# Gate factors over all vg steps, normalisation between the Strassen pairs, spatial weights early, output products fed block by block

## The chip, the cores and the metric

The kernel runs on one core of a Trainium2 chip. The metric is the device time of one execution in microseconds; the time given for a kernel is the median of its runs. The engines are named as the profile names them: PE is TensorE, DVE is VectorE, ACT is ScalarE, POOL is GpSimd, SP is SyncE. Each works through its own instructions in the order in which they stand in its stream.

## The reference

One layer of a hybrid trunk, with S = 512 tokens, D = 2048 channels, all in fp32:

```python
h = rms_norm(x, g_mix)
q, k, v_sb, u, v_sg, gate_a, gate_b = split(h @ w_in)      # 3 x 1024, 2 x 1024, 2 x 2048 columns
y_a = stick_breaking_attention(rms_norm(q), rms_norm(k), v_sb) @ w_oa     # 8 heads of 128
u = gelu(u); v_sg = gelu(v_sg)
v = layer_norm(v_sg, ln_g, ln_b)
mixed = einsum('gij,bcjgd->bcigd', masked(w_s), v) + b_s    # 8 groups, 4 chunks of 128 tokens
y_b = (u * mixed) @ w_ob
x = x + (sigmoid(gate_a) * y_a + sigmoid(gate_b) * y_b) @ w_out
x = x + square(relu(rms_norm(x, g_ff) @ w_ff1)) @ w_ff2
```

## The kernel before

**Products.** Every fp32 operand is split into a high and a low part (`split`, `split_to`, `weight`: ACT casts the high part, DVE subtracts to get the low part), and a product is three matmuls (`mm3`, L72 to L74). Weights come in pieces of 512 KB on SP's queue; their parts go into six buffers `w_piece`. Tiles of 128 x 512 come from one pool of slots, `slots`, and a smaller one, `long`; a new tile waits until the last user of an old one is done.

**Stages in order.** `by_token` makes q, k, v, then the vg columns (the gating unit's v), each in two halves of 512 columns; attention of a half runs beside the products that follow it. Then come `plain_pair` (two blocks of u as a plain product) and 19 `strassen_pair` (the rest of u, then both gates), which compute two column blocks by a Strassen scheme with sums of halves of h as moving operands; `factor` makes those sums, the "gate factors". Then `by_column` makes ya (from w_oa) and yb (from w_ob), then the output product and the feed-forward part, which the change leaves alone.

**Order of the work around a product.** A queue `behind` holds functions. After each weight piece `step()` runs the next one; `flush()` runs all that are left. What the functions emit goes to the engines through a scheduler, which sets the final order on each engine; `tc.issue_after(x)` keeps a transfer behind instruction x.

**Names.** `attention(half, ...)` gives 12 steps of `weights(h)` (scores and the weights `beta`), `turn(h)` (transposes `aT` on PE, split into `aT_hi`, `aT_lo`) and `product(h)` (the product `o`, split into `oT_hi`, `oT_lo`, stored to `held_o`). `save` has put h whole into `held_h`. `gate_factors(k)` fetches two tiles `whole` on POOL's queue and makes four sums, each a DVE operation (L241), an ACT one (L107 or L110) and a DVE one (L108 or L111). The evacuation of vg is a Gelu on ACT (L608). `normed(tb)` is the layer norm of 128 tokens: statistics on DVE, multiply and add on POOL (L637, L638), split on ACT and DVE into `vn`, two stores to `held_v` per half. `gated` multiplies a result by the row factor (L647, tile `act`), applies the activation (L648) and stores it to `held_g`. `spatial(half)` transposes four groups of w_s (`wsT`, L685) and splits them. `fetch_mix` fetches vn and u back, `mixed(g)` mixes one group (`mix`, `smix`) and splits it (`sT`). `evac_a` multiplies ya by a gate into `merged_a` (L737), for each of four column blocks; `gates` fetches the four gate tiles of a block.

In vg's 16 steps before, attention of the second half takes 12 and the eight gate factors the last four, two in each:

Of the kernel before, what the change touches and what calls it, by code (L numbers as in the profile page):

```python
# [16 lines left out]
P = 128  # L17
D = 2048
# [17 lines left out]
def tile_hybrid_layer(ctx: ExitStack, tc: tile.TileContext, x, g_mix, w_in, g_q, g_k, ln_g, ln_b,  # L36
# [29 lines left out]
    def f32(ap):  # L66
        return ap.bitcast(F32)
# [19 lines left out]
    def weight(wap, kt, c0, w=W):  # L87

        ck = CK * W // w
        raw = state["raw"].tile([P, ck, w], F32, name="w_raw", tag="w_raw")  # L90
        state["load"] = nc.sync.dma_start(
            out=raw, in_=wap[kt * P:(kt + ck) * P, c0:c0 + w].rearrange("(k p) c -> p k c", p=P))
        hi = wpool.tile([P, ck, w], F32R, name="w_hi", tag="w_piece", bufs=6)
        nc.scalar.copy(out=hi, in_=raw)  # L94
        lo = wpool.tile([P, ck, w], F32R, name="w_lo", tag="w_piece", bufs=6)
        nc.vector.tensor_tensor(out=lo, in0=raw, in1=f32(hi), op=ALU.subtract)  # L96
# [65 lines left out]
    class Sums:  # L162
# [15 lines left out]
        def parts(self, name):  # L178
            if name == "m7":
                nc.vector.tensor_tensor(out=self.a, in0=self.w11, in1=self.w21, op=ALU.add)  # L180
                if self.loaded:
                    nc.gpsimd.dma_start(out=self.w21, in_=self.blocks[1, 1], accum_op=ALU.add)  # L182
# [285 lines left out]

    held_h = dram.tile([KT, P, W], F32, name="held_h")
    held_o = dram.tile([HEADS, 2, P, W], F32, name="held_o")  # L470
    held_v = dram.tile([2, NTB, 2, P, W], F32, name="held_v")
    held_g = dram.tile([(SGW + 2 * D) // P, P, W], F32, name="held_g")
    scale = float(P) ** -0.5

# [110 lines left out]

# [9 lines left out]
    def gate_factors(k):  # L595
        whole = [fetched(held_h[2 * k + i], "whole") for i in range(2)]
        for name in ("m7", "m6", "m4", "m5"):
            factor(hy, whole, k, name, -1.0 if name in ("m7", "m4") else None)

    behind.extend([lambda k=k: (moved(2 * k), moved(2 * k + 1), moved(2 * k + 2), moved(2 * k + 3),  # L600
                                gate_factors(k), gate_factors(k + 1)) for k in range(0, KT // 2, 2)])

    vg = {}
    VS = 3 * SBW + SGW
# [15 lines left out]
                dst.append(t)  # L620
    vn = {}

    def normed(tb):
        st = tiny(12, "st")
        for half in range(2):
            nc.vector.bn_stats(out=st[:, half * 6:half * 6 + 6], in_=vg[tb, half])
# [4 lines left out]
        r = rsqrt(ve, 1, "r")  # L631
        for half in range(2):
            t = vg[tb, half]
            y = slot("y")
            nc.vector.tensor_scalar(out=y, in0=t, scalar1=mv[:, 0:1], scalar2=r, op0=ALU.subtract,
                                    op1=ALU.mult)
            nc.gpsimd.tensor_tensor(out=y, in0=y, in1=lng[half], op=ALU.mult)  # L637
            nc.gpsimd.tensor_tensor(out=y, in0=y, in1=lnb[half], op=ALU.add)  # L638
# [5 lines left out]
    def gated(n, act, func, signs, inside):  # L644
        for c, (t, sign) in enumerate(zip(act, signs)):
            a = t if inside else slot("act")
            nc.vector.tensor_tensor(out=a, in0=t, in1=rstd_b, op=ALU.mult)  # L647
            nc.scalar.activation(out=a, in_=a, func=func, scale=sign)  # L648
            nc.sync.dma_start(out=held_g[n + c], in_=a)

    US, GA = 3 * SBW, 3 * SBW + 2 * SGW
    order = [(US + n * P, n, AF.Gelu) for n in range(0, SGW // P, 2)]
    order += [(GA + n * P, SGW // P + n, AF.Sigmoid) for n in range(0, 2 * D // P, 2)]
    forks = None
    for c0, n, func in order:
        if forks is None:
            gated(n, plain_pair(win, c0, hy, "u"), func, (1.0, 1.0), False)
            flush()
            forks = new_forks(hy["y11", 0])
        else:  # L660
            gated(n, strassen_pair(win, c0, hy, forks), func, SIGNS, True)

    oT = [[fetched(held_o[h, i], "oT", F32R, long if h < LONG // 2 else slots) for i in range(2)]
          for h in range(HEADS)]

    def gates(which, j):
        n = SGW // P + which * (D // P) + j * 4
        return [fetched(held_g[n + c], "gate") for c in range(4)]
# [13 lines left out]
    def spatial(half):  # L682
# [11 lines left out]
        for i in range(2):  # L694
# [36 lines left out]
    ahead = gates(0, 0)  # L731
    for j in range(D // W):
        g, ahead = ahead, gates(0, j + 1) if j + 1 < D // W else gates(1, 0)

        def evac_a(c, o):
            m = slot("merged_a")
            nc.vector.tensor_tensor(out=m, in0=o, in1=g[c], op=ALU.mult)  # L737
# [4 lines left out]
    flush()
    mT = []
    for j in range(D // W):
        g, ahead = ahead, gates(1, j + 1) if j + 1 < D // W else None

        def evac_b(c, o):
            m = slot("merged")
            nc.vector.tensor_tensor(out=m, in0=o, in1=g[c], op=ALU.mult)
# [262 lines left out]
```

## Time and profile before

| | us |
|---|---|
| median of 3 runs | 2493.61 (2493.16 to 2493.72) |
| profiled execution | 2494.17 |
| its span | 2492.4 |
| PE busy in the span | 2428.3 |
| DVE, ACT, POOL busy | 1848.0, 1196.2, 467.9 |
| PE waits of over 1 us in the stages of the change | 18.6, 15.6, 2.6, 2.5, 2.5, 2.2, 2.1, 1.6, 1.1 |

A row of the timeline gives start, duration, engine, line, operation, output and input tiles, and in brackets how long the engine sat idle before it and what ended that. A row of the waits gives the total, how often, and the longest. A row of stretches gives the length, the busy time of PE, PE's weight loads, DVE, ACT and POOL with counts, then the clock granted to PE (1 is full), the busy share of the DMA engines and GB/s. A row of a group gives after the bar the busy time, the mean duration in ns and the idle time before. Stages in the profile of before: vg's second half with attention up to 415 us, u from 415 us, the first Strassen pair from 460 us, ya from 850 us.

### The profile page before, as it was taken

What the parts mean: (1) busy time and instruction counts of PE and PEld (TensorE: products, weight loads), DVE (VectorE), ACT (ScalarE), POOL (GpSimd) and SP (SyncE); (2) the same over time, 40 slices, a digit from 0 to 9 for tenths busy, and PEclk for the clock granted to TensorE, in tenths of its full rate; (3) what the DMA queues carried; (4) which work ended last, traced back from release to release, by engine and by line L of the source; (5) the groups of instructions that cost most, each with busy time, mean ns of one, the idle gap of its engine ahead of it and who ended that gap; (6) DMA issues with size and microseconds to landing.
All of it is one profiled execution on the core that took longest, in us unless ns stands there. A gap on an engine that the chain in (4) does not pass through costs nothing.

```text
span 2492.4 us, 34437 instructions
## 1 busy us (share of the span) xinstructions
PE 2428.3 (97%) x12696; PEld 2087.2 (84%) x12696; DVE 1848.0 (74%) x2416; ACT 1196.2 (48%) x1759; POOL 467.9 (19%) x590
## 2 busy tenths in 40 slices
PE   9999998699999989999999999999999999999999
PEld 7888887589888868888889888889888888888887
DVE  4566465777778644544679888888888899989887
ACT  5333343355555412322457777777765443333333
POOL 0223121610000331300000000000014435312210
PEclk9999999899999989999999999999999999999999
DMA  5243225666666853444459888898895999877763
GB/s 178 93 153 110 87 91 179 171 154 163 157 166 156 263 197 127 144 135 144 122 129 251 222 229 228 223 238 226 228 273 203 329 332 288 248 225 214 247 181 96
DMA packets 446122, 473.64 MB, mean 190 GB/s; under 512 B 20177, under 2 KB 328449, under 8 KB 445953
## 3 DMA queue, kind: packets, MB, share of 16 engines
q1 hardware_dynamic: 355984, 331.95, 41.7%
q0 software_dynamic: 89680, 138.97, 23.5%
q8 instruction: 100, 1.64, 0.3%
q10 hardware_dynamic: 288, 0.52, 0.1%
q14 instruction: 70, 0.57, 0.1%
HBM read 380.13 MB, written 90.18 MB: 189 GB/s over the span
## 4 chain that ended last, share of the span: by engine, by line
PE 61%; DVE 1%; DMA 0%; issue 0%; ACT 0%; POOL 0%; DVEq 0%
PE q L72 9%; PE q L73 9%; PE q L74 9%; PE q L214 7%; PE fork L214 7%; PE fork L217 4%; PE q L217 4%; PE xo L72 2%; PE xo L74 2%; PE xo L73 2%; PE yb L74 1%; PE yb L73 1%; PE yb L72 1%; PE ya L72 1%; PE ya L73 1%; PE ya L74 1%
## 5 line engine op out<-in xcount | busy, mean ns | idle before, releaser
L107 ACT CAST w_hi<-w_raw 128x1024 fp32r<-128x1024 f32 (+1 forms) x576 | 604.8, 1050 | 661.1 <-PE q L73 339.7
L108 DVE TENSOR_TENSOR w_lo<-w_raw,w_hi 128x1024 fp32r<-128x1024 f32 (+1 forms) x576 | 704.9, 1227 | 169.9 <-ACT w_hi L107 160.2
L73 PE MATMUL q<-w_lo,ys 128*128 128x512 f32 x896 | 348.8, 389 | 0.5 <-DVE w_lo L108 0.5
L96 DVE TENSOR_TENSOR w_lo<-w_raw,w_hi 128x1024 fp32r<-128x1024 f32 x135 | 168.9, 1251 | 243.1 <-ACT w_hi L94 239.1
L74 PE MATMUL q<-w_hi,ys 128*128 128x512 f32 x896 | 348.6, 389 | 0.0
L94 ACT CAST w_hi<-w_raw 128x1024 fp32r<-128x1024 f32 x135 | 141.8, 1050 | 373.0 <-issue 78.3
L72 PE MATMUL q<-w_hi,ys 128*128 128x512 f32 x896 | 312.0, 389 | 0.9 <-ACT w_hi L107 0.9
L214 PE MATMUL q<-ys,w_hi 128*128 128x512 f32 x1048 | 268.4, 393 | 2.5 <-ACT fork L221 2.5
L182 POOL DMA_DIRECT2D w_raw<-in_w_ff_dram x58 | 80.9, 1394 | 906.8 <-DVE m L844 343.4
L214 PE MATMUL fork<-ys,w_hi 128*128 128x512 f32 x896 | 224.9, 393 | 0.0
L214 PEld LDWEIGHTS q<-ys,w_hi 128*128 128x128 f32 x1048 | 186.9, 189 | 34.1 <-ACT fork L221 2.7
L73 PEld LDWEIGHTS q<-w_lo,ys 128*128 128x128 f32 x896 | 168.2, 188 | 36.4 <-DVE w_lo L108 1.5
L72 PEld LDWEIGHTS q<-w_hi,ys 128*128 128x128 f32 x896 | 168.1, 188 | 36.2 <-ACT w_hi L107 1.3
L74 PEld LDWEIGHTS q<-w_hi,ys 128*128 128x128 f32 x896 | 168.2, 188 | 34.9
L214 PEld LDWEIGHTS fork<-ys,w_hi 128*128 128x128 f32 x896 | 164.3, 190 | 31.1
L912 POOL DMA_DIRECT2D ys<-store x224 | 128.1, 609 | 175.6 <-PE q L74 117.9
L217 PEld LDWEIGHTS q<-ys,w_lo 128*128 128x128 f32 x1048 | 142.5, 190 | 10.4
L217 PE MATMUL q<-ys,w_lo 128*128 128x256 f32 x1048 | 145.7, 282 | 0.0
L72 PE MATMUL q<-ys,w_hi 128*128 128x256 f32 x400 | 114.4, 286 | 18.6 <-DVE act L647 18.6
L954 DVE SCALAR_TENSOR_TENSOR total<-q,plus,total 128x512 f32<-128x512 f32 x180 | 131.0, 744 | 0.4 <-PE q L74 0.4
L217 PEld LDWEIGHTS fork<-ys,w_lo 128*128 128x128 f32 x896 | 122.3, 190 | 8.6
L217 PE MATMUL fork<-ys,w_lo 128*128 128x256 f32 x896 | 125.3, 282 | 0.0
(293 smaller groups left out, 4732.5 us busy)
## 6 DMA issues: line engine op xcount, KB each, us to landing
w_raw<-in_w_ff_dram SPq DMA_DIRECT2D x256, 512.0 KB, 5.6
w_raw<-in_w_in_dram SPq DMA_DIRECT2D x143, 512.0 KB, 3.9
ys<-store POOLq DMA_DIRECT2D x224, 256.0 KB, 6.8
w_raw<-in_w_ff_dram POOLq DMA_DIRECT2D x58, 512.0 KB, 7.0
store<-ys_hi SPq DMA_DIRECT2D x90, 256.0 KB, 4.5
store<-ys_lo SPq DMA_DIRECT2D x90, 256.0 KB, 5.5
w_raw<-in_w_out_dram SPq DMA_DIRECT2D x32, 512.0 KB, 3.6
store<-ys SPq DMA_DIRECT2D x44, 256.0 KB, 6.3
```

The lines of the kernel that those rows point to most:

```text
L72: nc.tensor.matmul(o, lhsT=lh[0], rhs=rh[0], start=start, stop=False, **kw)
L73: nc.tensor.matmul(o, lhsT=lh[0], rhs=rh[1], start=False, stop=False, **kw)
L74: nc.tensor.matmul(o, lhsT=lh[1], rhs=rh[0], start=False, stop=stop, **kw)
L94: nc.scalar.copy(out=hi, in_=raw)
L96: nc.vector.tensor_tensor(out=lo, in0=raw, in1=f32(hi), op=ALU.subtract)
L107: nc.scalar.copy(out=hi, in_=src)
L108: state["lo"] = nc.vector.tensor_tensor(out=lo, in0=src, in1=f32(hi), op=ALU.subtract)
L182: nc.gpsimd.dma_start(out=self.w21, in_=self.blocks[1, 1], accum_op=ALU.add)
L214: nc.tensor.matmul(o, lhsT=hi[:, k, :], rhs=rhs[name][k], start=name == "y11" and k == 0, stop=False, skip_group_check=True)
L217: nc.tensor.matmul(o[:, :HS], lhsT=lo[:, k, :], rhs=rhs[name][k][:, :HS], start=False, stop=k == KH - 1, skip_group_check=True)
L912: nc.gpsimd.dma_start(out=f32(t), in_=store[f][HELD.index(name), p])
L954: nc.vector.scalar_tensor_tensor(out=a, in0=o, scalar=part, in1=a, op0=ALU.mult, op1=ALU.add)
```

## The change

- The eight gate factors stand at vg's steps 6, 8, 10, 11, 12, 13, 14 and 15, beside attention, which keeps steps 0 to 11; `moved` goes to steps 2 to 5.
- The layer norm is cut in two. `centred` (statistics and scaling, in place in the vg tile) runs for all tokens at u's first step. `normed(tb, half)` is POOL's multiply and add and one store, in every third step of the Strassen pairs. The split into vn parts is done after the fetch (`split_mix`), in ya. `held_v` holds one tile where it held two.
- `spatial` runs at u's third and fourth steps, where it ran at ya's start.
- The oT tiles of two heads are fetched ahead of the last pair, the others behind it into `long`.
- In ya and yb the fetches of vn, u and gates each stand behind a small POOL operation on the low part of the newest weight piece (`let`); `mixed(g)` stands at steps 5 to 8 and 10 to 13, and the flush between ya and yb is gone.

The diff's core (lines of after are one higher from L97 on):

```diff
     def weight(...):
         nc.vector.tensor_tensor(out=lo, in0=raw, in1=f32(hi), op=ALU.subtract)
+        state["piece"] = lo
...
-    held_v = dram.tile([2, NTB, 2, P, W], F32, name="held_v")
+    held_v = dram.tile([2, NTB, P, W], F32, name="held_v")
...
-        behind.extend(attention(half, qT, kT, v))
+        if half == 0:
+            behind.extend(attention(half, qT, kT, v))
...
-    behind.extend([lambda k=k: (moved(2 * k), moved(2 * k + 1), moved(2 * k + 2), moved(2 * k + 3),
-                                gate_factors(k), gate_factors(k + 1)) for k in range(0, KT // 2, 2)])
+    def at_steps(steps):
+        behind.extend([lambda fs=steps.get(i, []): [f() for f in fs] for i in range(max(steps) + 1)])
+
+    steps = collections.defaultdict(list)
+    for i, f in enumerate(attention(half, qT, kT, v)):
+        steps[i].append(f)
+    for k in range(KT):
+        steps[2 + k // 4].append(lambda k=k: moved(k))
+    for k, i in enumerate((6, 8, 10, 11, 12, 13, 14, 15)):
+        steps[i].append(lambda k=k: gate_factors(k))
+    at_steps(steps)
...
-    def normed(tb):
+    def centred(tb):
...
-            y = slot("y")
-            nc.vector.tensor_scalar(out=y, in0=t, scalar1=mv[:, 0:1], scalar2=r, op0=ALU.subtract,
+            nc.vector.tensor_scalar(out=t, in0=t, scalar1=mv[:, 0:1], scalar2=r, op0=ALU.subtract,
                                     op1=ALU.mult)
-            nc.gpsimd.tensor_tensor(out=y, in0=y, in1=lng[half], op=ALU.mult)
-            nc.gpsimd.tensor_tensor(out=y, in0=y, in1=lnb[half], op=ALU.add)
-            for i, part in enumerate(split(y, "vn")):
-                nc.gpsimd.dma_start(out=held_v[half, tb, i], in_=f32(part))
-
-    behind.extend([lambda tb=tb: normed(tb) for tb in range(NTB)])
+    def normed(tb, half):
+        t = vg[tb, half]
+        nc.gpsimd.tensor_tensor(out=t, in0=t, in1=lng[half], op=ALU.mult)
+        nc.gpsimd.tensor_tensor(out=t, in0=t, in1=lnb[half], op=ALU.add)
+        nc.gpsimd.dma_start(out=held_v[half, tb], in_=t)
...
+    behind.extend([lambda: [centred(tb) for tb in range(NTB)], lambda: None, lambda: spatial(0), lambda: spatial(1)])
...
             forks = new_forks(hy["y11", 0])
+            for tb in range(NTB):
+                for half in range(2):
+                    behind.extend([lambda tb=tb, half=half: normed(tb, half), lambda: None, lambda: None])
         else:
+            if (c0, n, func) == order[-1]:
+                with tc.issue_after(state["sum"].ins):
+                    for h in range(2):
+                        fetch_o(h, slots)
             gated(n, strassen_pair(win, c0, hy, forks), func, SIGNS, True)
+    with tc.issue_after(state["sum"].ins):
+        for h in range(2, HEADS):
+            fetch_o(h, long)
...
-            vn[tb, half] = [fetched(held_v[half, tb, i], "vn", F32R) for i in range(2)]
+            vn[tb, half] = fetched(held_v[half, tb], "vn")
...
+    def split_mix(half):
+        for tb in range(NTB):
+            vn[tb, half] = split(vn[tb, half], "vn")
...
-    behind.extend([lambda: (spatial(0), fetch_mix(0)), lambda: spatial(1)])
-    behind.extend([lambda g=g: (mixed(g), fetch_mix(1) if g == 1 else None) for g in range(GROUPS)])
+    def let(f):
+        gate = nc.gpsimd.tensor_tensor(out=tiny(4, "gate"), in0=f32(state["piece"])[:, 0, :4], in1=mhalf,
+                                       op=ALU.mult)
+        with tc.issue_after(gate.ins):
+            f()
+
+    with tc.issue_after(state["sum"].ins):
+        ahead = collections.deque([gates(0, 0)])
+    steps = collections.defaultdict(list)
+    steps[2].append(lambda: let(lambda: fetch_mix(0)))
+    steps[4].append(lambda: split_mix(0))
+    steps[6].append(lambda: let(lambda: fetch_mix(1)))
+    steps[9].append(lambda: split_mix(1))
+    for g in range(GROUPS):
+        steps[5 + g + g // 4].append(lambda g=g: mixed(g))
+    for i, wj in enumerate([(0, 1), (0, 2), (0, 3), (1, 0), (1, 1), (1, 2), (1, 3)]):
+        steps[4 * i].append(lambda wj=wj: let(lambda: ahead.append(gates(*wj))))
+    at_steps(steps)
...
-    flush()
+        ahead.popleft()
```

How the change moves instructions is shown at three places. The first is vg's first half with attention of the second. DVE before, from the last `beta` of `weights(3)` on:

```order
L540 SCALAR_TENSOR_TENSOR rest<-keep 128x128
L544 TENSOR_TENSOR beta<-beta,rest 128x127
L108 TENSOR_TENSOR oT_lo<-o,oT_hi 128x512
L108 TENSOR_TENSOR aT_lo<-aT,aT_hi 128x512
L108 TENSOR_TENSOR aT_lo<-aT,aT_hi 128x384
L108 TENSOR_TENSOR aT_lo<-aT,aT_hi 128x256
L108 TENSOR_TENSOR aT_lo<-aT,aT_hi 128x128
```

DVE now, from the same `beta` on (`whole` and `ys` are the operations of gate factor 0):

```order
L545 TENSOR_TENSOR beta<-beta,rest 128x127
L242 TENSOR_TENSOR whole<-whole 128x256 x2
L112 SCALAR_TENSOR_TENSOR ys<-whole,ys 128x256
L242 TENSOR_TENSOR whole<-whole 128x256
L109 TENSOR_TENSOR ys<-whole,ys 128x256
L242 TENSOR_TENSOR whole<-whole 128x256
L112 SCALAR_TENSOR_TENSOR ys<-whole,ys 128x256
L109 TENSOR_TENSOR ys<-whole,ys 128x256
L109 TENSOR_TENSOR oT_lo<-o,oT_hi 128x512
L109 TENSOR_TENSOR aT_lo<-aT,aT_hi 128x512
L109 TENSOR_TENSOR aT_lo<-aT,aT_hi 128x384
```

The eight DVE operations of factor 0 stand ahead of the `oT_lo` of `product(1)` and the `aT_lo` of `turn(2)`. POOL before, from the last `beta` multiplies of attention (the `whole` fetches are those of factor 0):

```order
L543 TENSOR_TENSOR beta<-beta,past 128x128 x4
L568 DMA held_o<-oT_hi 128x512
L568 DMA held_o<-oT_lo 128x512
L568 DMA held_o<-oT_hi 128x512
L568 DMA held_o<-oT_lo 128x512
L568 DMA held_o<-oT_hi 128x512
L477 DMA whole<-held_h 128x512 x2
```

POOL now, from the same multiplies:

```order
L544 TENSOR_TENSOR beta<-beta,past 128x128 x4
L478 DMA whole<-held_h 128x512 x2
L569 DMA held_o<-oT_hi 128x512
L569 DMA held_o<-oT_lo 128x512
L478 DMA whole<-held_h 128x512 x2
L569 DMA held_o<-oT_hi 128x512
```

The two fetches of factor 0 stand directly behind the last `beta` multiply, where they stood behind five stores of attention. The second place is ACT from u's third weight piece to the first Strassen pair. Before, the cast of that piece (the `w_hi` here) with the factor operations around it:

```order
L110 ACTIVATE ys<-whole 128x256
L107 CAST ys<-whole 128x256
L94 CAST w_hi<-w_raw 128x1024
L110 ACTIVATE ys<-whole 128x256
L107 CAST ys<-whole 128x256
L110 ACTIVATE ys<-whole 128x256
L107 CAST ys<-whole 128x256
```

Now, the casts of u's second and third pieces:

```order
L94 CAST w_hi<-w_raw 128x1024
L111 ACTIVATE ys<-whole 128x256
L94 CAST w_hi<-w_raw 128x1024
L108 CAST ys<-whole 128x256
L111 ACTIVATE ys<-whole 128x256
L108 CAST ys<-whole 128x256
```

The third cast stands inside factor 4, where it stood ahead of the third factor: 24 factor operations on ACT stood behind it before, 15 stand behind it now. Behind them, before, the evacuation of vg's second half and the first part of the pair:

```order
L107 CAST ys<-whole 128x256
L608 ACTIVATE vg<-vg,rstd 128x512 x4
L94 CAST w_hi<-w_raw 128x1024
L107 CAST w_hi<-w_raw 128x1024
L107 CAST vn_hi<-y 128x512
L107 CAST w_hi<-w_raw 128x1024 x2
L107 CAST vn_hi<-y 128x512
L107 CAST w_hi<-w_raw 128x1024
L221 COPY fork<-q 128x512
```

And now:

```order
L108 CAST ys<-whole 128x256
L618 ACTIVATE vg<-vg,rstd 128x512 x4
L94 CAST w_hi<-w_raw 128x1024
L108 CAST w_hi<-w_raw 128x1024 x2
L108 CAST wsp<-wsm 128x2x128
L108 CAST w_hi<-w_raw 128x1024
L108 CAST wsp<-wsm 128x2x128
L108 CAST w_hi<-w_raw 128x1024
L222 COPY fork<-q 128x512
L108 CAST wsp<-wsm 128x2x128 x2
L687 ACTIVATE act<-act 128x512
```

The casts of vn are gone, those of the spatial weights (`wsp`) and the first activation (`act`) stand there. The third place is DVE in ya. Before, at the end of the first column block (`merged_a`):

```order
L108 TENSOR_TENSOR sT_lo<-smix,sT_hi 128x512
L721 TENSOR_TENSOR smix<-mix,bs 128x256 x2
L723 TENSOR_TENSOR smix<-mix,smix 128x256 x2
L108 TENSOR_TENSOR sT_lo<-smix,sT_hi 128x512
L737 TENSOR_TENSOR merged_a<-ya,gate 128x512 x4
L721 TENSOR_TENSOR smix<-mix,bs 128x256 x2
```

And now, at the end of the second:

```order
L109 TENSOR_TENSOR sT_lo<-smix,sT_hi 128x512
L748 TENSOR_TENSOR smix<-mix,bs 128x256 x2
L750 TENSOR_TENSOR smix<-mix,smix 128x256 x2
L109 TENSOR_TENSOR sT_lo<-smix,sT_hi 128x512
L777 TENSOR_TENSOR merged_a<-ya,gate 128x512 x4
L748 TENSOR_TENSOR smix<-mix,bs 128x256 x2
L750 TENSOR_TENSOR smix<-mix,smix 128x256 x2
L109 TENSOR_TENSOR sT_lo<-smix,sT_hi 128x512
```

An `sT_lo` still stands directly ahead of `merged_a` there; at the end of the first block none does.

More of the change, by code (lines that the diff above doesn't have):

```diff
@@ L181, in parts @@
                 if self.loaded:
-                    nc.gpsimd.dma_start(out=self.w21, in_=self.blocks[1, 1], accum_op=ALU.add)
+                    state["sum"] = nc.gpsimd.dma_start(out=self.w21, in_=self.blocks[1, 1], accum_op=ALU.add)
             if name == "m6":
@@ L633, in normed @@
             t = vg[tb, half]
-            y = slot("y")
-            nc.vector.tensor_scalar(out=y, in0=t, scalar1=mv[:, 0:1], scalar2=r, op0=ALU.subtract,
+            nc.vector.tensor_scalar(out=t, in0=t, scalar1=mv[:, 0:1], scalar2=r, op0=ALU.subtract,
                                     op1=ALU.mult)
-            nc.gpsimd.tensor_tensor(out=y, in0=y, in1=lng[half], op=ALU.mult)
-            nc.gpsimd.tensor_tensor(out=y, in0=y, in1=lnb[half], op=ALU.add)
-            for i, part in enumerate(split(y, "vn")):
-                nc.gpsimd.dma_start(out=held_v[half, tb, i], in_=f32(part))
-    behind.extend([lambda tb=tb: normed(tb) for tb in range(NTB)])
[L644 to L657, printed above, removed]
-            flush()
[L659 to L668, printed above, removed]
+    def normed(tb, half):
[3 more added lines that the diff above has]
+        nc.gpsimd.dma_start(out=held_v[half, tb], in_=t)
     wsT = []
@@ L698, in spatial, with gated, fetch_o, gates @@
             wsT.append(pair)
+    def gated(n, act, func, signs, inside):
+        for c, (t, sign) in enumerate(zip(act, signs)):
+            a = t if inside else slot("act")
+            nc.vector.tensor_tensor(out=a, in0=t, in1=rstd_b, op=ALU.mult)
+            nc.scalar.activation(out=a, in_=a, func=func, scale=sign)
+            nc.sync.dma_start(out=held_g[n + c], in_=a)
+    US, GA = 3 * SBW, 3 * SBW + 2 * SGW
+    order = [(US + n * P, n, AF.Gelu) for n in range(0, SGW // P, 2)]
+    order += [(GA + n * P, SGW // P + n, AF.Sigmoid) for n in range(0, 2 * D // P, 2)]
+    behind.extend([lambda: [centred(tb) for tb in range(NTB)], lambda: None, lambda: spatial(0), lambda: spatial(1)])
+    forks = None
+    oT = []
+    def fetch_o(h, pool):
+        oT.append([fetched(held_o[h, i], "oT", F32R, pool) for i in range(2)])
+    for c0, n, func in order:
+        if forks is None:
+            gated(n, plain_pair(win, c0, hy, "u"), func, (1.0, 1.0), False)
+            flush()
+            forks = new_forks(hy["y11", 0])
+            for tb in range(NTB):
+                for half in range(2):
+                    behind.extend([lambda tb=tb, half=half: normed(tb, half), lambda: None, lambda: None])
+        else:
+            if (c0, n, func) == order[-1]:
+                with tc.issue_after(state["sum"].ins):
+                    for h in range(2):
+                        fetch_o(h, slots)
+            gated(n, strassen_pair(win, c0, hy, forks), func, SIGNS, True)
+    with tc.issue_after(state["sum"].ins):
+        for h in range(2, HEADS):
+            fetch_o(h, long)
+    def gates(which, j):
+        n = SGW // P + which * (D // P) + j * 4
+        return [fetched(held_g[n + c], "gate") for c in range(4)]
     sT = []
@@ L725, in mixed @@
         sT.append(split(t, "sT"))
[L727 to L728 removed]
+    def let(f):
[15 more added lines that the diff above has]
+    at_steps(steps)
     merged_a = []
[L731 removed]
     for j in range(D // W):
[L733 removed]
         def evac_a(c, o):
             m = slot("merged_a")
[L737 removed]
+            nc.vector.tensor_tensor(out=m, in0=o, in1=ahead[0][c], op=ALU.mult)
             merged_a.append(m)
         by_column(w_oa[0], j * W, lambda k: oT[k], SBW // P, evac_a, "ya")
[L742 removed]
+        ahead.popleft()
     mT = []
     for j in range(D // W):
[L745 removed]
         def evac_b(c, o):
             m = slot("merged")
[L749 removed]
+            nc.vector.tensor_tensor(out=m, in0=o, in1=ahead[0][c], op=ALU.mult)
             nc.gpsimd.tensor_tensor(out=m, in0=m, in1=merged_a[j * 4 + c], op=ALU.add)
@@ L753, in tile_hybrid_layer @@
         by_column(w_ob[0], j * W, lambda k: sT[k], SGW // P, evac_b, "yb")
+        ahead.popleft()
     EARLY = 6
```

## The prediction

> **What bounds the kernel now.** I read the engine table first, then the list of what TensorE waited for, then the table of stretches with the granted clock, and last the timeline around each long wait. First the span, and the one engine that fills it:
>
> ```profile
> span 2492.4 us, 34437 instructions
> PE 2428.3 (97%) x12696; PEld 2087.2 (84%) x12696; DVE 1848.0 (74%) x2416; ACT 1196.2 (48%) x1759; POOL 467.9 (19%) x590
> ```
>
> TensorE works 97% of the span; 64.1 us of it are idle. The edits take away no large product, so what they can bring is idle time, and matmuls that run at a low clock after it. Who it waits for (total, times, longest):
>
> ```profile
> PE q L72 <- DVE act L647: 18.6, 1, 18.6
> PE u L72 <- ACT vg L608: 15.6, 1, 15.6
> PE ya L72 <- DVE merged_a L737: 5.0, 2, 2.5
> PE mix L717 <- DVE smix L723: 3.9, 2, 2.2
> PE wsT L685 <- DMA ws<-in_w_spatial_dram: 2.6, 1, 2.6
> PE u L72 <- DMA hT<-hT_both: 2.1, 1, 2.1
> PE ya L74 <- DVE w_lo L96: 1.1, 1, 1.1
> ```
>
> These seven, 48.9 us, lie in the code that the change touches. The rest (the first load and single waits elsewhere) is left. After each such wait the same matmuls take longer:
>
> ```profile
> 443.73 0.58 PE L72 MATMUL u<-hT,w_hi 128*128 128x256 f32 x1 [15.60 <-ACT vg L608]
> 449.02 0.30 PE L72 MATMUL u<-hT,w_hi 128*128 128x256 f32 x1
> 449.51 0.28 PE L73 MATMUL u<-hT,w_hi 128*128 128x256 f32 x1
> 449.63 0.28 PE L74 MATMUL u<-hT,w_lo 128*128 128x256 f32 x1
> 927.74 0.80 PE L72 MATMUL ya<-oT,w_hi 128*128 128x512 f32 x1 [2.51 <-DVE merged_a L737]
> 933.45 0.53 PE L73 MATMUL ya<-oT,w_hi 128*128 128x512 f32 x1
> 933.82 0.39 PE L74 MATMUL ya<-oT,w_lo 128*128 128x512 f32 x1
> 430.00:460.00 30.00, 16.27 (x116) 16.27 (x117) 21.66 (x46) 10.58 (x20) 10.70 (x13) 0.72 0.43 107
> 920.00:940.00 20.00, 15.25 (x63) 12.50 (x62) 9.34 (x19) 2.91 (x4) 5.93 (x7) 0.83 0.21 69
> ```
>
> From 443.73 to 449.02 there are 24 matmuls, 0.220 us apart, and then 0.120: 24 x 0.10 = 2.4 us lost after one gap. From 927.74 to 933.82 there are 14 matmuls, 0.43 us apart; with the same near doubling about 0.2 of each is lost, 2.9 in all, though that gap was only 2.51 us. The stretches show it as granted clocks of 0.72 and 0.83. So I price a restart at 2.4. [...]
>
> **Part 1: gate factors over the vg steps.** Before, the eight factors stand after attention, and the evacuation of vg's second half stands on ACT behind the last of them; the second bank of u needs that bank:
>
> ```profile
> 415.08 1.05 ACT L94 CAST w_hi<-w_raw 128x1024 fp32r<-128x1024 f32 x1 [2.72 <-issue]
> 417.31 0.88 DVE L241 TENSOR_TENSOR whole<-whole 128x256 f32<-128x256 f32 x2
> 421.62 0.88 DVE L241 TENSOR_TENSOR whole<-whole 128x256 f32<-128x256 f32 x2
> 443.00 2.41 ACT L608 ACTIVATE vg<-vg,rstd 128x512 f32<-128x512 f32 x4
> ```
>
> One factor is a chain between DVE and ACT of 4.3 us (417.31 to 421.62). Vg's last matmul ends at 415.07 (call it T). In the new order k1 to k3 lie on an idle DVE before T (half busy: 20.3 of 40 us between 360 and 400), but on ACT the w_hi cast of u's third weight, which waits for vg's last matmul, stands in the middle of k4, with the rest of k4 and k5 to k7 behind it. So the evacuation is done at T + 1.05 (that cast) + 2.45 (rest of k4) + 3 x 4.35 + 0.6 (one evacuation) + about 0.5 = T + 17.7, where it was T + 28.7. TensorE now has u's whole first bank ahead of it: 72 matmuls x 0.120 = 8.6. A wait of 9.1 replaces 15.6 + 2.1.
>
> Factor k0 is put earlier than its data allows. On DVE its eight instructions stand behind the last `beta` of `weights(3)` and ahead of the `oT_lo` of `product(1)` and the `aT_lo` of `turn(2)`; its fetch is issued on POOL only behind the last `beta` multiply of `weights(3)`:
>
> ```profile
> 366.11 0.61 POOL L543 TENSOR_TENSOR beta<-beta,past 128x128 f32<-128x128 f32 x1 [1.47 <-ACT beta L536]
> 394.91 1.08 POOL L477 DMA_DIRECT2D whole<-held_h  x2
> 401.37 0.89 DVE L241 TENSOR_TENSOR whole<-whole 128x256 f32<-128x256 f32 x2 [6.56 <-DMA whole<-held_h]
> DMA to landing us min/median/max: 2.7/5.2/6.9
> 368.77 0.68 DVE L108 TENSOR_TENSOR oT_lo<-o,oT_hi 128x512 fp32r<-128x512 f32 x1
> 369.72 0.71 PE L554 MATMUL aT<-ident,beta 128*128 128x128 f32 x3
> 360.00:400.00 40.00, 39.86 (x200) 33.55 (x199) 20.29 (x32) 17.45 (x30) 9.51 (x16) 1.00 0.39 123
> ```
>
> The fourth row is of the `whole` fetches. The second fetch is issued at about 366.72 + 0.54 = 367.3; at 4.5 us (between minimum and median, since only two are sent and DMA is at 0.39) it lands at 371.8, k0 ends at 376.1 and `oT_lo` at 376.8. TensorE wanted to go on with `aT` at 369.72, and the next vg matmuls stand behind `aT` and `o`. That is a new wait of 7.1 us (5.3 with the minimum, 9.5 with the maximum) plus a restart of 2.4: 9.5. This stretch is all busy at full clock before. Together: 17.7 + 9.5 = 27.2 against 28.7, so u's second bank starts 1.5 us earlier. Costs at restart stay: 2.4 before and after.
>
> **Part 2: normalisation, spatial weights, first gating.** Before, q's first product waits 18.6 us, because the `act` multiply stands on DVE behind all eight vn splits, which follow POOL's multiply and add one by one:
>
> ```profile
> 501.76 0.55 PE L72 MATMUL q<-ys,w_hi 128*128 128x256 f32 x1 [18.64 <-DVE act L647]
> L638 POOL TENSOR_TENSOR y<-y,lnb 128x512 f32<-128x512 f32 x8 | 14.1, 1764 | 0.6
> L637 POOL TENSOR_TENSOR y<-y,lng 128x512 f32<-128x512 f32 x8 | 13.2, 1650 | 0.1
> held_v<-vn_hi POOLq DMA_DIRECT2D x8, 256.0 KB, 3.6
> 448.34 1.27 POOL L637 TENSOR_TENSOR y<-y,lng 128x512 f32<-128x512 f32 x1
> 473.26 2.16 POOL L638 TENSOR_TENSOR y<-y,lnb 128x512 f32<-128x512 f32 x1
> ```
>
> The splits go out of this chain, but `act` takes its slot from a vg tile whose store is the second on POOL. Counted from u's second bank (R): first multiply at R + 4.6 (448.34 - 443.73), ten multiplies and adds of 1.79 (mean of the groups with a gap of 0.08), small `r` operations, a weight accumulate and the issues, store at about R + 25, landed 3.6 to 4.2 later at R + 29. Behind it on ACT stand both gating activations and two weight casts; the fork copy that TensorE needs comes at R + 34.5. TensorE gets there at R + 29.8. So a wait of 4.8 (0 to 9), and 1.3 for a shorter restart, in place of 18.6 + 2.4. The eight wsT transposes and the fork work inside u add 1.9. Gain 21.0 - 4.8 - 1.3 - 1.9 = 13.0. The fetch of ws decides a side wait:
>
> ```profile
> ws<-in_w_spatial_dram SPq DMA_DIRECT2D x2, 256.0 KB, 16.8
> xk<-in_x_dram SPq DMA_DIRECT2D x4, 256.0 KB, 5.1
> 850.00:880.00 30.00, 26.32 (x121) 21.37 (x120) 12.85 (x23) 8.37 (x13) 11.82 (x22) 0.94 1.04 383
> ```
>
> The 16.8 us were taken at a DMA share of 1.04; with 0.4 to 0.7 in the new place I take the 5.1 of the other row of 256 KB, which is hidden. The shorter and longer POOL operations (1.27 and 2.16) are the bounds of the chain: ten times 0.4 either way. [...]
>
> **Part 3: the ya products.** Waits before: 2.6 (ws), 1.1 (w_lo), 1.6 and 2.2 (smix), 2.5 and 2.5 (merged_a), 12.5 in sum, and 6.4 at a low clock (2.9 and 2.4 after the `merged_a` gaps, 1.1 after the ws gap, each from the spacing of the matmuls behind it). The ws wait and the smix waits go: the transposes have moved (1.1 of matmul time with them), and `mixed` is spread with empty steps between. The `merged_a` wait stays at two boundaries of column blocks, since `sT_lo`, which waits for ACT, still stands ahead of it on DVE:
>
> ```profile
> 893.29 0.69 DVE L108 TENSOR_TENSOR sT_lo<-smix,sT_hi 128x512 fp32r<-128x512 f32 x1 [2.03 <-ACT sT_hi L107]
> 900.00:920.00 20.00, 20.00 (x97) 16.73 (x96) 8.61 (x14) 5.24 (x6) 4.56 (x6) 1.00 0.56 203
> ```
>
> I leave 2.7 and 1.5 there and 2.1 for the clock. Gain 12.5 + 6.4 + 1.1 - 6.3 = 13.7. The vn splits (8 x 0.7 on DVE, 8 x 0.6 on ACT) fall into the ya stage, where DVE is busy 8.6 of 20 us (last row). Half the vn transfers go, and the oT fetches come earlier; DMA bounds nothing here. The POOL operation that holds back a fetch until a weight's low part is there reads a piece whose buffer is needed three weights later, some 16 us; POOL's work between is under 6 us. Nothing for these.
>
> **Sum.** 1.5 + 13.0 + 13.7 = 28.2. The profiled execution took 2494.17, so 2466.0; it lies 0.56 over the median of 2493.61, so the median becomes 2465.4.
>
> **Rivals.**
> - All waits go: k0's fetch comes in time, the slot is free, the boundaries pass. Then 48.9 of idle and 2.4 + 2.4 + 6.4 of clock, less 1.9 for work moved into u: 2494 - 58 = 2435. Against it stands the order on DVE and ACT.
> - One more wait in u: ws lands after 16.8 as before (about 5.6 more, since the act wait covers a part) or POOL's ten operations take 2.16 each (3.7 more): 2469 to 2475.
> - The early factors cost more: k1's eight instructions stand ahead of a w_lo and of the next `oT_lo`, its fetch behind a store that waits for k0's end. If TensorE runs out of weights there too, another 7.1 + 2.4: 2475, and for k2 as well 2484. The half-busy DVE speaks against it.
> - The factors gain nothing because k0's wait grows to the maximum, and `act` and the boundaries stay as late as before: 2489 to 2494, no change.
> - Slower, by one mechanism: POOL's holding operations. Seven of them stand in POOL's queue between gate fetches and smix multiplies. If w_lo's buffer waits for POOL each time, DVE stops, and with it all weights. Above 28.2 / 7 = 4.0 us each this decides; at the 8 us of a full wait for a landing (the longest here 6.9) and an issue it is 56 us: 2521. Against it: three weights of slack.
>
> **Chances.** Forecast as worked out 0.58; all waits gone 0.10; one more wait in u 0.12; more early waits 0.06; no change 0.07; slower 0.07. A run can tell about 0.2%, 5 us, from no change: below 2488.6 is faster (0.58 + 0.10 + 0.12 + 0.06 = 0.86), up to 2498.6 the same (0.07), above it slower (0.07). The range runs from 2446, where k0's wait (9.5), the act wait (6.1) and the boundary waits (4.2) are all gone and only the wait for u's second bank is left, to 2490, which takes in the second and third rivals and part of the fourth. The likeliest case alone is 2458 to 2473.
>
> **What would show it.** Right: a wait of `aT` or `o` of about 7 us near 370, released by DVE `oT_lo`; u's second bank waiting for ACT vg about 9 us; no wait of 18 us for `act`, and one below 9 before the first pair's second product; in ya only `merged_a` waits. Wrong: no gap near 370, ws in the list with more than 3 us, DVE w_lo waiting for POOL in ya, or a wait in the gate pairs, where the chance of POOL holding up weights would have been set too low.

## The result, and the profile after

The median fell from 2493.39 us (2490.9 to 2493.72) to 2468.25 us (2467.88 to 2469.41): a ratio of 0.9902, 95% interval 0.9885 to 0.9919. The forecast was 2465.4 in a range of 2446 to 2490. The waits of TensorE, longest in total first (total, times, longest):

```profile
PE fork L288 <- DVE wsm L674: 12.8, 2, 9.4
PE u L72 <- ACT vg L618: 8.9, 1, 8.9
PE aT L555 <- DVE oT_lo L109: 6.8, 1, 6.8
PE gp L367 <- DMA gm<-in_g_mix_dram: 5.8, 1, 5.8
PE q L215 <- ACT fork L222: 2.5, 1, 2.5
PE ya L72 <- DVE merged_a L777: 1.8, 2, 1.5
```

The 18.6 for `act` is gone, as are the waits for `smix`, `wsT` and `hT`. The second and third rows are the two that the forecast named, at 9.1 and 7.1. The first row is larger than anything it had there. By stage, from the first matmul of each product in the two traces:

| stretch | before, us | after, us | gained | forecast |
|---|---|---|---|---|
| to u's first matmul | 415.1 | 423.7 | -8.7 | -9.5 |
| from there to u's second bank | 28.7 | 17.7 | 11.0 | 11.0 |
| u's second bank to ya | 407.9 | 403.5 | 4.4 | 13.0 |
| ya to yb | 119.0 | 99.8 | 19.2 | 13.7 |
| yb to the end | 1521.8 | 1523.0 | -1.2 | 0 |

The sum, 24.7, is the difference of the spans (2492.4 and 2467.7). The last row lies within noise: that stretch takes 1521.1 to 1523.0 us in the profiles of this case. The new wait ahead of u, in the timeline (start, duration, then idle before and its cause):

```profile
366.52 1.13 POOL L478 DMA_DIRECT2D whole<-held_h  x2
371.52 0.88 DVE L242 TENSOR_TENSOR whole<-whole 128x256 f32<-128x256 f32 x2 [2.49 <-DMA whole<-held_h]
375.93 0.69 DVE L109 TENSOR_TENSOR oT_lo<-o,oT_hi 128x512 fp32r<-128x512 f32 x1
376.68 1.07 PE L555 MATMUL aT<-ident,beta 128*128 128x128 f32 x3 [6.79 <-DVE oT_lo L109]
441.43 0.58 PE L72 MATMUL u<-hT,w_hi 128*128 128x256 f32 x1 [8.91 <-ACT vg L618]
```

The second of the two fetches was issued at about 367.1, half of the 1.13 behind 366.52, and factor 0 began at 371.52, about 4.4 us later; the forecast took 4.5. Then DVE, POOL and TensorE at the end of u, where the large wait is:

```profile
463.83 0.43 DVE L674 COPY wsm<-wsT 64x256 f32<-64x256 f32 x1
464.79 9.91 DVE L109 TENSOR_TENSOR wsp<-wsm,wsp 128x256 fp32r<-128x256 f32 x1 [0.53 <-ACT wsp L108]
475.76 0.41 DVE L109 TENSOR_TENSOR wsp<-wsm,wsp 128x256 fp32r<-128x256 f32 x1
462.33 1.67 POOL L183 DMA_DIRECT2D w_raw<-in_w_in_dram  x1
465.15 3.27 POOL L649 TENSOR_TENSOR vg<-vg,lng 128x512 f32<-128x512 f32 x2
468.23 3.19 POOL L650 TENSOR_TENSOR vg<-vg,lnb 128x512 f32<-128x512 f32 x2
471.24 3.17 POOL L650 TENSOR_TENSOR vg<-vg,lnb 128x512 f32<-128x512 f32 x2
464.41 0.47 PE L288 MATMUL fork<-hT 128*128 128x512 f32 x1 [3.40 <-DVE wsm L674]
477.82 0.76 PE L288 MATMUL fork<-hT 128*128 128x512 f32 x1 [9.36 <-DVE wsm L674]
```

One DVE operation of 0.41 us took 9.91 and ended at 474.7, 0.3 us behind POOL's last add (474.4). Behind it on DVE stood the copy that frees the PSUM bank for the second fork, and TensorE stands at the fork: that is the wait of 9.36. The first fork's wait, 3.40, lies ahead of the long operation. The copy at 463.83, whose input is in PSUM, was not held up: it took 0.43 us beside POOL's add (2.00 us from 463.30), as the same copy did at 477.24, with POOL's operations done. The scaling operations of `centred`, which read one tile and two values per row, were slowed: they took 1260 ns on average, where they take 542 in the run further down that has no multiplies and adds on POOL (first line the changed kernel, second line that run):

```profile
L644 DVE TENSOR_SCALAR vg<-vg,mv,r 128x512 f32<-128x512 f32 x8 | 9.8, 1260 | 0.0
L644 DVE TENSOR_SCALAR vg<-vg,mv,r 128x512 f32<-128x512 f32 x8 | 4.0, 542 | 0.0
```

In ya the first boundary of column blocks shows no wait, the next two 1.54 and 0.26, and the granted clock is 1.00 from 890 to 920:

```profile
900.80 0.50 PE L72 MATMUL ya<-oT,w_hi 128*128 128x512 f32 x1 [1.54 <-DVE merged_a L777]
926.39 0.50 PE L72 MATMUL ya<-oT,w_hi 128*128 128x512 f32 x1 [0.26 <-DVE merged_a L777]
890.00:920.00 30.00, 28.46 (x140) 23.92 (x139) 16.45 (x29) 9.02 (x13) 7.45 (x9) 1.00 0.46 158
```

### The profile page after: what moved, and what is told of

Same layout as the page of the kernel before. It is cut to its first block, busy times and chain, and to the rows that moved or that the text cites. A ratio compares the mean times of both kernels' runs of the same rounds, so it can differ in the third digit from the quotient of the medians.

```text
span 2467.7 us, 34420 instructions
## 1 busy us (share of the span) xinstructions
PE 2422.0 (98%) x12696; PEld 2082.2 (84%) x12696; DVE 1857.9 (75%) x2416; ACT 1196.6 (48%) x1759; POOL 450.8 (18%) x583
## 4 chain that ended last, share of the span: by engine, by line
PE 94%; DVE 3%; issue 1%; DMA 1%; ACT 1%; POOL 0%; DVEq 0%; SPq 0%; ACTq 0%; POOLq 0%
PE q L215 11%; PE fork L215 11%; PE q L73 11%; PE q L72 11%; PE q L74 11%; PE fork L218 6%; PE q L218 6%; PE xo L72 2%; PE xo L73 2%; PE xo L74 2%; PE v L74 1%; PE v L72 1%; PE v L73 1%; PE yb L74 1%; PE yb L72 1%
## 5 line engine op out<-in xcount | busy, mean ns | idle before, releaser
L183 POOL DMA_DIRECT2D w_raw<-in_w_ff_dram x58 | 80.9, 1395 | 908.0 <-DVE m L883 413.5
L181 DVE TENSOR_TENSOR w_raw<-w_raw 128x1024 f32<-128x1024 f32 x82 | 101.3, 1236 | 26.7 <-DMA w_raw<-in_w_ff_dram 10.3
```

## The experiments

All start from the changed kernel, 2468.25 us. The kernel before ran again beside the changed kernel and beside each group of them, with medians from 2491.25 to 2493.39 us, so a difference of 2 us between two medians shows nothing by itself; the stretches of the traces are given beside them where they say more.

**Is it POOL that holds DVE?** The first takes one of the two SBUF inputs away from the held operation, the second takes POOL's work away.

```diff
-            split_to(p3[:, :, 0, :], p3[:, :, 1, :], m3[:, 2 * i:2 * i + 2, :])
...
+            nc.scalar.copy(out=hi, in_=m3[:, part, :])
+            nc.scalar.copy(out=lo[64:, :, :64], in_=m3[64:, part, :64])
...
+            nc.vector.tensor_tensor(out=lo[:64], in0=t3[:64, part, :], in1=f32(hi[:64]), op=ALU.subtract)
+            nc.vector.tensor_tensor(out=lo[64:, :, 64:], in0=t3[64:, part, 64:], in1=f32(hi[64:, :, 64:]), op=ALU.subtract)
```

(`hi` and `lo` are the two parts of the pair, `t3` is the transposed weights in PSUM.)

> Changed kernel, with the low parts of the spatial weights subtracted from the transposes in PSUM, so that this DVE operation has one input in SBUF where it had two (the zero corner is written by ACT). Theory: the 9.91 us operation was held off by POOL's multiplies and adds, because both its inputs lie in SBUF. Then each of the new subtractions takes under 1 us although POOL runs on, the wait of 9.4 us for the second fork goes, and what is left is a wait for the first activation's slot of 2 to 5 us: 2461 us (2457 to 2465). Rival: the operation is slow by itself (its output is written in strips of 128 elements) or waits for something that the trace does not show: it stays near 10 us and the time at 2468 (2466 to 2471).

Measured: 2466.6 us. The expected time was missed; the mechanism shows nevertheless. DVE in this kernel's timeline:

```profile
464.50 0.42 DVE L684 TENSOR_TENSOR wsp<-wsT,wsp 64x256 fp32r<-64x256 f32 x1 [0.47 <-ACT wsp L681]
464.93 0.29 DVE L685 TENSOR_TENSOR wsp<-wsT,wsp 64x128 fp32r<-64x128 f32 x1
465.45 9.74 DVE L109 TENSOR_TENSOR w_lo<-w_raw,w_hi 128x1024 fp32r<-128x1024 f32 x1 [0.22 <-ACT w_hi L108]
```

The operations with one input in SBUF take 0.42 and 0.29 while POOL works (its add runs from 463.06 to 465.06, its next multiply from 464.93). The next with two, a weight's low part that took 1.21 us at 454.07, takes the whole hold instead, 9.74. Its output is not written in strips, so the shape of the output was not the cause, and mending one operation only passed the hold on: TensorE waited 11.5 us for the fork.

The second kernel leaves out the gain and the bias of the layer norm:

```diff
-        nc.gpsimd.tensor_tensor(out=t, in0=t, in1=lng[half], op=ALU.mult)
-        nc.gpsimd.tensor_tensor(out=t, in0=t, in1=lnb[half], op=ALU.add)
```

> Changed kernel without POOL's sixteen multiplies and adds of the layer norm (gain and bias are left out; the stores stay). Theory: DVE's subtraction for the spatial weights takes 0.4 us, the weight subtractions there 1.2, and both waits of the forks (3.4 and 9.4) shrink to under 1.5 each; the slot of the first activation is free early: 2453 us (2450 to 2458). Rival (slow by itself): 9.9 us and 2468 as before.

Measured: 2451.72 us, and no wait of the forks' matmuls for DVE is left. The four `wsp` subtractions take 415 to 426 ns. POOL's sixteen operations cost 16.5 us of time, 15.2 of it between u's second bank and ya (388.3, after 403.5); with the first experiment this shows them as the cause.

**What is in front of u?**

```diff
-    for k, i in enumerate((6, 8, 10, 11, 12, 13, 14, 15)):
+    for k, i in enumerate((8, 8, 10, 11, 12, 13, 14, 15)):
```

> Changed kernel with gate factor 0 at vg step 8 beside factor 1, where it stood at step 6: on DVE it now stands behind the low parts of product(1) and turn(2). Theory: the wait of 6.8 us at 370 us and its slow restart go, so u starts at about 415 where it started at 423.7; but 4.5 factors stand behind the cast of u's third weight, where 3.75 did, so the wait for vg's evacuation grows from 8.9 to about 12: 2463 us (2460 to 2466). Rival: the factor stops DVE as much one step later, the wait moves behind the next turn: 2468 (2466 to 2471).

Measured: 2461.42 us. The wait at 370 us is gone, and the wait for vg's evacuation is 11.9. Factor 0's early place cost 6.8 us net; in the traces u's second bank starts 7.3 earlier (434.1, after 441.4). Then all factors back in vg's last four steps, two in each, as before the change:

```diff
-    steps = collections.defaultdict(list)
...
-    for k, i in enumerate((6, 8, 10, 11, 12, 13, 14, 15)):
-        steps[i].append(lambda k=k: gate_factors(k))
-    at_steps(steps)
+    behind.extend(attention(half, qT, kT, v))
+    behind.extend([lambda k=k: (moved(2 * k), moved(2 * k + 1), moved(2 * k + 2), moved(2 * k + 3),
+                                gate_factors(k), gate_factors(k + 1)) for k in range(0, KT // 2, 2)])
```

> Changed kernel with the gate factors back at vg's last four steps, two in each; all else as changed. Theory: the spread gains 10.9 us behind vg (28.7 to about 17.7 from vg's end to u's second bank) and loses 8.6 ahead of it (factor 0's wait of 6.8 and its restart). Undone: no wait at 370 us, u starts at 415, its second bank at 443.7 after a wait of 15 to 18: 2470.5 us (2468.5 to 2473). Rival: factor 0's wait costs as much as the spread gains, or more: 2466 to 2468.

Measured: 2470.8 us (2467.34 to 2472.09), with 15.7 and 2.4 in front of u's second bank. By the medians the spread as it was made gains 2.6 us, by the start of u's second bank 1.3 (442.8 and 441.4): little more than runs differ by, so this hardly tells it from the rival, no gain at all. With factor 0 at step 8 it gains 9.4.

**Where does ya's gain come from?** The feeding of ya and yb is put back, with vn still split after its fetch:

```diff
...
-    for g in range(GROUPS):
-        steps[5 + g + g // 4].append(lambda g=g: mixed(g))
-    for i, wj in enumerate([(0, 1), (0, 2), (0, 3), (1, 0), (1, 1), (1, 2), (1, 3)]):
-        steps[4 * i].append(lambda wj=wj: let(lambda: ahead.append(gates(*wj))))
-    at_steps(steps)
+    behind.extend([lambda: fetch_mix(0), lambda: split_mix(0)])
+    behind.extend([lambda g=g: (split_mix(1) if g == 4 else None, mixed(g), fetch_mix(1) if g == 1 else None)
+                   for g in range(GROUPS)])
+    blocks = collections.deque([(0, 1), (0, 2), (0, 3), (1, 0), (1, 1), (1, 2), (1, 3)])
+    ahead = collections.deque([gates(0, 0)])
...
     for j in range(D // W):
+        ahead.append(gates(*blocks.popleft()))
...
+    flush()
...
     for j in range(D // W):
+        if blocks:
+            ahead.append(gates(*blocks.popleft()))
```

> Changed kernel with the feeding of ya and yb as before the change: no holding POOL operations, mixed(g) in successive steps from the third on, gates fetched at the start of each column block, the flush between ya and yb; vn is still stored whole and split after the fetch, and the spatial weights stay in u. Theory: the spread of mixed(g) is what took the merged_a and smix waits away. They come back, 1.1 + 1.6 + 2.2 + 2.5 + 2.5 of idle and 5.3 of low clock less the 1.8 left now: 2482 us (2477 to 2487). Rival: the wait for the transposes and the full DMA queues at ya's start were the cause of them all, and both are gone with the moved spatial weights: 2468 to 2471.

Measured: 2475.27 us, less than expected. From ya's first matmul to yb's it took 107.5 us (843.1 to 950.6), where after the change it takes 99.8 and before 119.0. So the spread of `mixed` and of the fetches is worth 7.7 of the 19.2; the rest came with the steps that this kernel kept. The waits for `smix` came back in full, one of the two for `merged_a` did, at 1.7:

```profile
PE mix L744 <- DVE smix L750: 3.8, 2, 2.9
PE ya L72 <- DVE merged_a L772: 1.7, 1, 1.7
```

Next the two spatial steps go back to ya, their loads still early:

```diff
-    behind.extend([lambda: [centred(tb) for tb in range(NTB)], lambda: None, lambda: spatial(0), lambda: spatial(1)])
+    behind.extend([lambda: [centred(tb) for tb in range(NTB)]])
...
+    steps[0].append(lambda: spatial(0))
+    steps[1].append(lambda: spatial(1))
```

> Changed kernel with the two spatial steps back at ya's first two steps (their loads stay early). Theory: u's end then has no spatial work for POOL's run to hold up, but the low part of a weight stands there instead, and behind it the first activation waits for its slot until about 29 us after u's second bank, which was the forecast's own term: TensorE waits 5 to 8 us in the first pair where it waits 12.8 for the forks; ya, with its transposes but without a wait for their load, takes 1 to 3 us more: 2463.5 us (2460 to 2467). Rival: spatial work at ya's start brings back the waits of ya as they were (5 us or more there): 2468 to 2474.

Measured: 2464.45 us: 3.8 faster than with the steps in u. By the traces, from u's second bank to ya it takes 398.7 us, 4.8 less, and ya takes 100.5 with them, 0.7 more. So what helped ya was not that the transposes left it. If the parts add, the other 10.8 of ya's 19.2 lie in steps that no run here separates: the earlier loads of ws and oT, vn stored whole and split behind its fetch. DVE in u:

```profile
461.95 0.68 DVE L686 TENSOR_TENSOR act<-u,rstd_b 128x512 f32<-128x512 f32 x1
462.55 12.11 DVE L109 TENSOR_TENSOR w_lo<-w_raw,w_hi 128x1024 fp32r<-128x1024 f32 x1
```

The first activation did not wait for its slot at all: it ran at 461.95, 21.4 us after u's second bank (440.58). The forecast had put the free slot at 29. (In the changed kernel this can't be read: there the activation, at 479.29, stands behind the held operation.) Again the next operation with two SBUF inputs took the hold, and TensorE waited 7.8 for it.

**Why six operations and not one?** Earlier in the same stage of the changed kernel DVE and POOL take turns: DVE's subtraction, 1.21 us at 454.33, takes 2.28 at 460.58. To see whether the stores between POOL's operations matter, they went to SP's queue:

```diff
-        nc.gpsimd.dma_start(out=held_v[half, tb], in_=t)
+        nc.sync.dma_start(out=held_v[half, tb], in_=t)
```

> Changed kernel with the eight stores of the normalised vg tiles issued on SP's queue instead of POOL's; POOL's multiplies and adds stay where they are, without a store between them. It asks why one DVE operation with two SBUF inputs waited through six POOL operations (9.9 us), while others earlier in the same stage waited through one (2.3 us). Theory A: the DMA issues between POOL's operations keep DVE out. Then no DVE operation there takes over 3.5 us, and the wait of the second fork falls from 9.4 to below 4: 2462 us (2459 to 2465). Theory B: operations that are ready back to back on POOL do so by themselves: one DVE operation takes 7 to 11 us again, 2467 (2465 to 2470).

Measured: 2467.46 us; a DVE operation was held for 11.00 us, through seven POOL operations. So theory A falls and B fits:

```profile
461.94 11.00 DVE L109 TENSOR_TENSOR w_lo<-w_raw,w_hi 128x1024 fp32r<-128x1024 f32 x1
461.58 1.64 POOL L183 DMA_DIRECT2D w_raw<-in_w_in_dram  x1
466.31 5.54 POOL L650 TENSOR_TENSOR vg<-vg,lnb 128x512 f32<-128x512 f32 x4
```

The held operation ends 1.1 us, about its own time, behind POOL's last one (at 472.94, after 471.85): this fits that it ran when POOL was done. B does not say why DVE and POOL took turns at 445 to 461 us, though. In the holds of 9.91, 9.74 and 11.00 us POOL had issued a weight accumulate (L183, at 462.33, 462.08 and 461.58) and went on with its operations behind it; the next run shows that this alone is not enough, and what decides stays open.

**Two ways out.** The operations go behind the accumulates of the second to fourth pair, or to DVE itself.

```diff
-        nc.gpsimd.tensor_tensor(out=t, in0=t, in1=lng[half], op=ALU.mult)
-        nc.gpsimd.tensor_tensor(out=t, in0=t, in1=lnb[half], op=ALU.add)
-        nc.gpsimd.dma_start(out=held_v[half, tb], in_=t)
+        with tc.issue_after(state["sum"].ins):
+            nc.gpsimd.tensor_tensor(out=t, in0=t, in1=lng[half], op=ALU.mult)
+            nc.gpsimd.tensor_tensor(out=t, in0=t, in1=lnb[half], op=ALU.add)
+            nc.gpsimd.dma_start(out=held_v[half, tb], in_=t)
...
             forks = new_forks(hy["y11", 0])
+            behind.extend([lambda: None] * 7)
```

> Changed kernel with POOL's multiplies, adds and stores tied behind the weight accumulate of the second to fourth Strassen pair, two tiles or fewer after each. Theory: nothing holds DVE off while u ends, so the forks' waits go (12.8 and 2.4); what the operations hold up later is short, since DVE works ahead of TensorE there; but activations that take a slot of a vg tile now wait for its later store: 2457 us (2452 to 2464). Rival: the slots, or the held off weight subtractions, cost as much in the pairs: 2465 to 2475.

Measured: 2467.04 us: the rival. The hold moved into the pairs with the operations, on the sum of two weights:

```profile
472.72 7.11 DVE L185 TENSOR_TENSOR w_raw<-w_raw 128x1024 f32<-128x1024 f32 x1
498.81 6.55 DVE L185 TENSOR_TENSOR w_raw<-w_raw 128x1024 f32<-128x1024 f32 x1
521.05 9.39 DVE L185 TENSOR_TENSOR w_raw<-w_raw 128x1024 f32<-128x1024 f32 x1
```

Each ended 1.1 us behind the last of the four, four and six POOL operations that ran beside it. The first group in this run also stands directly behind an accumulate (issued at 450.87), but it is one tile's multiply and add, the second of which needs the first. There DVE's sum ends 1.1 us behind the first, at 454.9, and the second takes 2.17: DVE got its turn after one operation:

```profile
451.86 1.97 POOL L650 TENSOR_TENSOR vg<-vg,lng 128x512 f32<-128x512 f32 x1
452.05 2.87 DVE L185 TENSOR_TENSOR w_raw<-w_raw 128x1024 f32<-128x1024 f32 x1 [0.66 <-DMA w_raw<-in_w_in_dram]
453.92 2.17 POOL L651 TENSOR_TENSOR vg<-vg,lnb 128x512 f32<-128x512 f32 x1
```

The second way puts the operations on DVE:

```diff
-        nc.gpsimd.tensor_tensor(out=t, in0=t, in1=lng[half], op=ALU.mult)
-        nc.gpsimd.tensor_tensor(out=t, in0=t, in1=lnb[half], op=ALU.add)
+        nc.vector.tensor_tensor(out=t, in0=t, in1=lng[half], op=ALU.mult)
+        nc.vector.tensor_tensor(out=t, in0=t, in1=lnb[half], op=ALU.add)
```

> Changed kernel with the layer norm's sixteen multiplies and adds on DVE instead of POOL. Theory (POOL's operations hold DVE off, DVE's own work has room): DVE gets 16 x 0.69 = 11 us more work but no operation there takes over 1.3 us, both waits of the forks shrink below 2 each, the first activation's slot is free early; some u or pair weights come late by up to 4: 2456 us (2452 to 2461). Rival (DVE is full in this stage whoever does the norm): TensorE waits for low parts of weights as long as it now waits for the forks, 2465 to 2470.

Measured: 2454.18 us. The sixteen operations take 10.7 us on DVE, and 14.1 us of time are saved, 13.9 of them between u's second bank and ya:

```profile
L650 DVE TENSOR_TENSOR vg<-vg,lnb 128x512 f32<-128x512 f32 x8 | 5.4, 686 | 0.0
L649 DVE TENSOR_TENSOR vg<-vg,lng 128x512 f32<-128x512 f32 x8 | 5.3, 685 | 0.0
```

With factor 0 at step 8 as well (that edit and this one together):

> Changed kernel with both repairs: multiplies and adds of the norm on DVE, gate factor 0 at vg step 8. Theory: the two causes are independent, so the gains add: 2454.2 - 6.8 = 2447.4 us (2445 to 2450), with a wait of about 12 us for vg's evacuation as the only one over 3 us in this stage. Rival: DVE, full from u on, cannot take the earlier start: 2450 to 2454.

Measured: 2449.67 us, at the upper end of what was expected, next to the rival: the gains nearly add, 18.6 where both together make 20.9.

**The last wait.** With both repairs in place, factors 6 and 7 go to u's first two steps, behind vg's evacuation; then the same with the spatial steps in ya, by the edit shown above.

```diff
-    for k, i in enumerate((6, 8, 10, 11, 12, 13, 14, 15)):
+    for k, i in enumerate((8, 8, 10, 12, 13, 14)):
...
-    behind.extend([lambda: [centred(tb) for tb in range(NTB)], lambda: None, lambda: spatial(0), lambda: spatial(1)])
+    behind.extend([lambda: (gate_factors(6), [centred(tb) for tb in range(NTB)]), lambda: gate_factors(7), lambda: spatial(0), lambda: spatial(1)])
```

> As the kernel with both repairs, and gate factors 6 and 7 at u's first two steps, so that the evacuation of vg stands ahead of them on ACT. Theory: the wait for the evacuation falls by two factors of 4.35 from 12 to about 3.5, and the 7 us of DVE work that moves behind it finds room: 2440 us (2437 to 2445). Rival: DVE is full there, and low parts of weights come late by what was gained: 2446 to 2452.

Measured: 2448.69 us, the rival's time. The wait for the evacuation fell to 3.1, and u's second bank starts 9.0 us earlier than with both repairs alone; but from there to ya it takes 398.5 us, where it took 390.2, so nearly all of it is lost again. The first pair now waits for the late factors (the longest wait is for `ys`, not for a weight's low part as the rival had it), and then runs at a low clock:

```profile
457.95 0.51 PE L72 MATMUL q<-ys,w_hi 128*128 128x256 f32 x1 [2.67 <-ACT ys L111]
460.00:480.00 20.00, 18.60 (x95) 15.92 (x96) 18.44 (x31) 11.80 (x22) 1.61 (x1) 0.79 0.50 119
```

> Everything that helped at once: norm on DVE, factor 0 at vg step 8, factors 6 and 7 in u, spatial steps at ya's start. Theory: what the two factors in u lost before was DVE's room (full from 420 to 480 us); the spatial work that leaves u gives DVE back 5 us and TensorE the transposes, so the small waits of the first pair (2.7, 0.7, 0.6, 0.6) and the low clock behind them shrink: 2442 us (2438 to 2446). Rival: the last factor's chain between ACT and DVE sets these waits, not DVE's load: 2446 to 2449.

Measured: 2448.4 us (2447.66 to 2450.1), ratio to before 0.9825 (0.9809 to 0.9842): the fastest median, though no better than the one ahead of it beyond their spread. The wait for `ys`, which ends at 458, stayed, at 3.6. DVE's load fell only behind that wait (15.9 us busy of 460 to 480, after 18.4): ahead of it DVE is busy for 18.5 of the 20 us from 440 to 460, after 18.3. So the run doesn't tell the last factor's chain from DVE's want of room, and that stays open.

## Why the prediction was right, and where not

The direction, the two places in front of u and the total (24.7 gained in the span, 28.2 forecast) held. Point by point:

- **Factors.** The forecast put factor 0's wait at 7.1 and a restart of 2.4; measured 6.79 and 1.9 (8.7 less the wait). It put 17.7 us from vg's end to u's second bank; measured 17.7. The runs with factor 0 at step 8 and with all factors at their old places bear out both.
- **Normalisation and spatial weights.** This step failed: 13.0 forecast, 4.4 measured. The term "a wait of 4.8 (0 to 9)" for the activation's slot was the wrong one: in the run with the spatial steps in ya the activation ran 21.4 us after u's second bank without a wait for a slot. In its place stood 12.8 us of waits for the forks, 9.4 of them behind one DVE operation held for 9.91. One of the forecast's own signs failed with it: it wanted a wait below 9 before the pair's second product. The second of its rivals lengthened POOL's operations to 2.16 us each, but had no DVE operation wait for them. In the run with one of the inputs in PSUM such an operation was not held (0.42 and 0.29 us beside POOL's operations); the scaling operations, with one tile and two values per row from SBUF, took 1260 ns beside POOL's operations and 542 without them, so two tiles were not needed for a slowdown. The hold of 9.91 us went through six POOL operations (465.15 to 474.4).
- **ya.** 13.7 forecast, 19.2 measured. The terms left there, 2.7 + 1.5 and 2.1 for the clock, were too large: 1.54 + 0.26, and a granted clock of 1.00 from 890 to 920. That is 4.5 of the 5.5 that were missed.
- **Cancelling.** One part was 8.6 too high and the other 5.5 too low. The total came closer than its parts, 2.9 us from the forecast, and that is luck: the two errors lie in different stages and have different causes.
- **Hidden costs.** The ws fetch landed in 2.9 us in its new place, so its rival is out, and no weight waited for POOL in ya: its only wait there is `merged_a`, 1.8. The slower rival is out too.

## What to carry to other kernels

When work on GpSimd is gathered into one run, look for every DVE operation with two SBUF inputs beside it: here one that started in such a run paid for the run's whole rest, 9.91 us where 0.41 is its own time, and DVE was the cheaper place for that work, by 14.1 us. Look at operations with one tile from SBUF too: the scaling took 1260 ns, where it took 542 without POOL's work. A step put early in a queue is only as early as its own fetch, as factor 0 was, at a wait of 6.79 us; leave it behind what the next matmul needs. Check a forecast stage by stage, since a total can agree by errors that cancel.

## What the hardware showed that was not expected

A DVE operation was held through whole runs of POOL operations: 9.91, 9.74, 11.00 and 7.11 us where 0.41 to 1.23 is its own time. Elsewhere it got its turn after one of them, at 2.28 or 2.87. And the clock did not follow the length of a gap alone: a gap of 2.51 us before the change was followed by 6 us with matmuls 0.43 us apart, where the same ones came 0.23 apart behind them (granted clock 0.51 from 927.7 to 933.9, then 1.00), while after it the one of 3.40 us at 464.41 was followed by matmuls 0.12 us apart until the next gap (granted clock 1.00 from 464.4 to 468.3):

```profile
464.71 0.99 PE L218 MATMUL q<-hT,w_lo 128*128 128x256 f32 x7
465.54 0.28 PE L72 MATMUL q<-ys,w_hi 128*128 128x256 f32 x1
468.18 0.28 PE L73 MATMUL q<-ys,w_hi 128*128 128x256 f32 x1
```

What decides the clock behind a gap, these runs do not show.
